# First projection tiles, the z stores and the gated unit's buffers in a two-layer decoder trunk

## The chip, the core and the metric

The kernel runs on one core of one Trainium2 chip. The metric is the device time of one execution in microseconds (us); lower is better.

## The reference, cut to what matters

x is 1024 positions by 1024 channels. Layer 0 is a state-space layer, layer 1 is differential attention:

```
xn = rmsnorm(x, g);  u, z = split(xn @ in_w)          # in_w: 1024 x 2048, u columns first
y  = s5_ssm(u, ...) + d_skip * u                       # 64 groups of 16 channels, 64 complex states each
y  = gelu(y)
y  = y * sigmoid(y @ glu_w + glu_b)                    # the gated unit
h  = x + (y * silu(z)) @ out_w
# layer 1: keys and values from h, queries and gate from h, attention, out-projection, final norm
```

The scan needs u. z is read only behind the gated unit, so it can be computed and stored at any time before.

## The kernel before, in words

Everything is held transposed: 128 channels on the partitions, 1024 positions along the free dimension, in 8 tiles (`KT`). A float32 product is split into three matmuls (`mm3`, lines 159 to 161): a rounded high part and a rest of each operand, hi*hi, hi*lo and lo*hi. A tile of a dense projection (`dense`) is 8 steps of k by two halves of 512 positions by 3, that is 48 matmuls into two PSUM banks. The pool `ps` has four banks, `ps2` two. Weights come by `load_m`: SyncE loads 512 KB into `mraw` (one buffer), ScalarE rounds them into `mhi` (line 749), VectorE takes the difference `mlo` (line 750); `mhi` and `mlo` have two buffers each.

The program is written as straight code and a planner orders the instructions of each engine at build time, by the order of the text, the buffers that are free, and its own estimate of each duration. Each engine and each DMA queue then runs its list in order.

Layer 0 begins with three tiles for which the weights come in pieces (`fw`), so that matmuls can start k by k while x arrives. Beside them run the sums of squares for the norm: matmuls of line 526, a ScalarE copy (530), small matmuls (532), `rcol` (534, 535), `norm_rows` (688) and a ScalarE copy into R (537). The norm is applied on evacuation: for tiles of u, VectorE multiplies the accumulator by R (line 491) and SyncE stores it (492). Tiles of z are copied as they are by ScalarE (494) and stored by SyncE (495); R comes in later, in the gated unit. Both go through `evo`, a ring of two buffers.

Then `ssm_setup` computes tables on VectorE (C3, B3, D, ES3, ET4 in pool `ssm`). `ORDER` lists the scan stage in the text's order: for each of the 8 groups of tiles, t and c make tables (`bt`, `bT`, `ca`, `toep`), u projects a tile, a feeds the scan (`ug`, `pb`), o computes y and ScalarE's queue stores it to `yd` (439). The tiles of z stand at the end of the text, and the planner takes them as filler. The gated unit (`glu`) loads y back (`load_y`, line 595): y0 early into a buffer of its own, y1 to y7 into `yr`, which uses the stream buffers tagged "ya", "sg" and "z", two of each. It casts them to `yh` (610) and `yl` (611), multiplies by `glu_w`, and its `done` reads z and y again and writes `y2h` and `y2l`. `yh` and `yl` take the memory of `xh` and `xl`. In memory the pool of y2 came first, above it the stream buffers `cd`, then `cd1`, where the pools of the scan stage had been.

Of the kernel before, what the change touches and what calls it, by code (L numbers as in the profile page):

```python
# [8 lines left out]
F32 = mybir.dt.float32  # L9
# [9 lines left out]
P = 128  # L19
SEQ = 1024  # L20
D = 1024
KT = D // P
# [11 lines left out]
NEG = -1e30  # L34


ORDER = ("t0 c0 t1 u3 a0 c1 o0 t2 u4 a1 c2 o1 t3 u5 a2 c3 o2 t4 u6 a3 c4 o3 t5 u7 a4 c5 o4 t6 a5 c6 o5 t7 a6 c7 o6 a7 "
         "o7").split()


# [14 lines left out]
class Trunk:  # L55
# [389 lines left out]
    def layer0(self, dbg=None):  # L445
        tc, nc, I = self.tc, self.nc, self.I
        V, G, S = nc.vector, nc.gpsimd, nc.scalar
        dr = self.dr
        ps = self.ps
# [9 lines left out]
        with ExitStack() as es:  # L459
            sp, ev = pool(es, "ssm", 1), pool(es, "ev", 2)  # L460
            stp = ExitStack()
            tp = pool(stp, "stp", 1)
            R = self.R1
            pcr = self.ps3.tile([P, 2, 512], F32, name="pb")
            sqs = []

            pick = tp.tile([P, 2], F32, name="pick")
            G.memset(pick, 0.0)
            for r in range(4):
                G.memset(pick[32 * r:32 * r + 1, r // 2:r // 2 + 1], 1.0)  # L470

            ga = tp.tile([P, KT], F32, name="ga")
            nc.sync.dma_start(ga, I["ga"])

            def prep_x(k, cuts):
                raw = tp.tile([P, SEQ], F32, name="xraw", bufs=3)
                g = ga[:, k:k + 1]
                for c in cuts:
                    nc.sync.dma_start(raw[:, c], I["xT"][k * P:(k + 1) * P, c])
                    S.activation(xh[k][:, c], raw[:, c], AF.Copy, scale=g)  # L480
                    V.scalar_tensor_tensor(xl[k][:, c], raw[:, c], g, rd(xh[k][:, c]), op0=ALU.mult,
                                           op1=ALU.subtract)
                sqs.append(tp.tile([P, SEQ], F32, name="rt0", bufs=3))
                S.activation(sqs[k], raw, AF.Square)

            def evac(m, pt):
                for h in range(2):
                    hs = slice(h * 512, h * 512 + 512)
                    o = ev.tile([P, 512], F32, name="evo")
                    if m < KT:  # L490
                        V.tensor_mul(o, pt[h], R[:, hs])  # L491
                        nc.sync.dma_start(udv[m][:, hs], o)
                    else:
                        S.copy(o, pt[h])
                        nc.sync.dma_start(zds[m - KT][:, hs], o)


            pt0 = [[(ps if m < 2 else self.ps2).tile([P, 512], F32, name="ps") for h in range(2)] for m in range(3)]
            fst = ExitStack()
            fp = pool(fst, "first", 1)  # L500
            fw = []
            for k in range(KT):
                raw = fp.tile([P, 3 * P], F32, name="fw", bufs=3)
                hi = fp.tile([P, 3 * P], F32R, name=f"fh{k}")
                lo = fp.tile([P, 3 * P], F32R, name=f"fl{k}")
                nc.sync.dma_start(raw, I["in_w"][k * P:(k + 1) * P, 0:3 * P])
                S.copy(hi, raw)
                V.tensor_sub(lo, raw, rd(hi))
                prep_x(k, (slice(0, 512), slice(512, SEQ)) if k == 0 else (slice(0, SEQ),))
                if k == 0:  # L510
                    self.load_consts()
                    for i, pl in enumerate((tp, sp)):
                        self.load_small(i, pl.tile([P, CUTS[i + 1] - CUTS[i]], F32, name=f"small{i}"))
                fw.append((hi, lo))
            def first_u(k):
                for m in range(3):
                    ms = slice(m * P, (m + 1) * P)
                    self.mm_tile((fw[k][0][:, ms], fw[k][1][:, ms]), pt0[m], xh, xl, k)

            late = KT - 2  # L520
            for k in range(KT):
                if k < late:
                    first_u(k)
                for h in range(2):
                    r = 64 * h + k % 2 * 32
                    nc.tensor.matmul(pcr[r:r + 32, 0, :], self.ones.broadcast_to([P, 32]),
                                     sqs[k][:, h * 512:h * 512 + 512], start=k < 2, stop=k >= KT - 2,
                                     tile_position=(0, r))
            part = tp.tile([P, SEQ], F32, name="rt0", bufs=3)[:, 0:512]
            S.copy(part, pcr[:, 0, :])  # L530
            for q in range(KT):
                nc.tensor.matmul(pcr[:, 1, q:q + 1], part[:, q % 4 * P:(q % 4 + 1) * P], pick[:, q // 4:q // 4 + 1],
                                 start=True, stop=True)
            S.activation(self.rcol, pcr[:, 1, 0:KT], AF.Identity, bias=self.small1[:, 5:6], scale=1.0 / D)
            G.tensor_tensor(self.rcol, self.rcol, self.mhalf.broadcast_to([P, KT]), op=ALU.pow)
            self.norm_rows([pcr[:, q // 4, q % 4 * P:(q % 4 + 1) * P] for q in range(KT)], self.rcol)
            S.copy(R, pcr.rearrange("p h c -> p (h c)"))
            for k in range(late, KT):
                first_u(k)
            fst.close()  # L540
            for m in range(3):
                evac(m, pt0[m])
            self.ssm_setup(sp, tp)
            V.memset(self.small1[:, 2:3], SUBLN_EPS)
            V.tensor_scalar(self.small1[:, 0:1], self.sm("subln"), 1.0 - LAM_INIT, None, op0=ALU.mult)
            V.tensor_scalar(self.gq, self.sm("gb"), 0.125, None, op0=ALU.mult)
            stp.close()
            yst = ExitStack()
            yq = yst.enter_context(tc.tile_pool(name="yq", bufs=YQ, side="right", reuse_waits="tile"))
            sb, tb = pool(es, "ssb", 2), pool(es, "sst", 1)  # L550
            self.ks = tb.tile([P, T, P], F32, name="ks")
            G.memset(self.ks, 0.0)
            psb = self.ps3
            t = {}
            ops = {
                "t": lambda b: t.update({b: self.ssm_in(b, sb, tb, self.ps2)}),
                "c": lambda b: self.ssm_tables(b, t[b], sb, tb, self.ps2, dr),
                "u": lambda b: self.dense(I["in_w"], (b,), xh, xl, ps, evac),
                "a": lambda b: self.ssm_apply(b, t[b], sb, tb, psb, uds[b]),
                "o": lambda b: self.ssm_out(b, t[b], tb, self.ps2, yds[b]),  # L560
            }
            for x in ORDER:
                ops[x[0]](int(x[1]))
            self.yraw = []
            for k in range(YQ):
                self.yraw.append(yq.tile([P, SEQ], F32, name="yq"))
                self.load_y(yds, k, self.yraw[k])
            self.dense(I["in_w"], range(8, 16), xh, xl, ps, evac)
        with ExitStack() as es:
            yp, cd, cd1 = pool(es, "y2p", 1), pool(es, "cd", 2), pool(es, "cd1", 1)  # L570
            self.glu(yp, cd, ps, yds, zds)
            yst.close()
            self.out0(cd, cd1, ps)
# [8 lines left out]
            hs = slice(h * 512, h * 512 + 512)  # L582
            self.mm3(pt[h], w[0], w[1], xh[k][:, hs], xl[k][:, hs], k == 0, k == KT - 1)

    def dense(self, src, tiles, xh, xl, ps, done, gain=None):

        for m in tiles:
            wh, wl = self.load_m(src, 0, KT, m * P, P, gain)
            pt = [ps.tile([P, 512], F32, name="ps") for h in range(2)]
            for k in range(KT):  # L590
                self.mm_tile((wh[:, k, :], wl[:, k, :]), pt, xh, xl, k)
            done(m, pt)
# [4 lines left out]
    def glu(self, yp, cd, ps, yds, zds):  # L597
# [19 lines left out]
        def done(m, pt):  # L617
            z = cd.tile([P, SEQ], F32, name="z")
            nc.sync.dma_start(z, zds[m])
            sg = cd.tile([P, SEQ], F32, name="sg")  # L620
            a = cd.tile([P, SEQ], F32, name="ya")
            self.load_y(yds, m, a)
            G.tensor_mul(z, z, self.R1)
            G.tensor_mul(a, a, z)
            S.activation(z, z, AF.Sigmoid)
            for h in range(2):
                hs = slice(h * 512, h * 512 + 512)
                S.activation(sg[:, hs], pt[h], AF.Sigmoid, bias=self.sm("glub")[:, m:m + 1])
            V.tensor_mul(sg, sg, z)
            V.tensor_mul(sg, sg, a)  # L630
            S.copy(self.y2h[m], sg)
            V.tensor_sub(self.y2l[m], sg, rd(self.y2h[m]))

        self.dense(I["glu_w"], range(8), yh, yl, ps, done)

    def out0(self, cd, cd1, ps):
        nc, I = self.nc, self.I
# [541 lines left out]
```

## Time and profile before

| | us |
|---|---|
| median of 3 runs (1092.6 to 1092.8) | 1092.7 |
| the profiled execution, its own time | 1093.5 |
| its span, first to last instruction | 1091.7 |
| TensorE busy | 1061.9 |
| VectorE busy | 822.5 |
| ScalarE busy | 623.9 |
| GpSimd busy | 235.3 |
| granted TensorE clock, mean | 0.991 |

The span is the time between the first and the last instruction on the core; the execution's own time has 1.8 us around it. In the rows, PE is TensorE, DVE VectorE, ACT ScalarE, POOL GpSimd, SPq and ACTq the queues by which SyncE and ScalarE issue transfers. L491 is line 491 of the kernel. Busy times of matmuls overlap, so steps between their starts are the better measure. A wait for several things is put down to the one that came last.

### The profile page before, as it was taken

What the parts mean: (1) busy time and instruction counts of PE and PEld (TensorE: products, weight loads), DVE (VectorE), ACT (ScalarE), POOL (GpSimd) and SP (SyncE); (2) the same over time, 40 slices, a digit from 0 to 9 for tenths busy, and PEclk for the clock granted to TensorE, in tenths of its full rate; (3) what the DMA queues carried; (4) which work ended last, traced back from release to release, by engine and by line L of the source; (5) the groups of instructions that cost most, each with busy time, mean ns of one, the idle gap of its engine ahead of it and who ended that gap; (6) DMA issues with size and microseconds to landing.
All of it is one profiled execution on the core that took longest, in us unless ns stands there. A gap on an engine that the chain in (4) does not pass through costs nothing. (4 is left out here: it accounts for less than half of the span.)

```text
span 1091.7 us, 17715 instructions
## 1 busy us (share of the span) xinstructions
PE 1061.9 (97%) x6308; PEld 908.2 (83%) x6308; DVE 822.5 (75%) x1617; ACT 623.9 (57%) x1396; POOL 235.3 (22%) x237
## 2 busy tenths in 40 slices
PE   7999999999999999999999999999999999899996
PEld 5678888887788888998888898889988898788896
DVE  7789999984577543547898778877698777987475
ACT  6432343332534332436787788767788778785463
POOL 0000000000356112211222122221222222210258
PEclk9999999999899999999999999999999999999998
DMA  8143546544654445313122212222222222553344
GB/s 283 45 136 116 174 151 174 159 151 133 238 193 135 127 140 157 135 42 90 44 85 57 73 56 66 86 56 78 66 53 79 60 84 61 148 175 105 109 134 159
DMA packets 143143, 125.94 MB, mean 115 GB/s; under 512 B 9808, under 2 KB 123216, under 8 KB 143056
## 3 DMA queue, kind: packets, MB, share of 16 engines
q1 hardware_dynamic: 134736, 120.63, 36.0%
q10 hardware_dynamic: 8320, 4.19, 1.3%
q8 instruction: 49, 0.80, 0.3%
q14 instruction: 38, 0.31, 0.1%
HBM read 85.48 MB, written 33.03 MB: 109 GB/s over the span
## 5 line engine op out<-in xcount | busy, mean ns | idle before, releaser
L159 PE MATMUL pm<-h1h,mhi 128*128 128x512 f32 x352 | 139.5, 396 | 1.0 <-DVE xr L767 1.0
L160 PE MATMUL pm<-h1l,mhi 128*128 128x512 f32 x352 | 138.8, 394 | 0.0
L161 PE MATMUL pm<-h1h,mlo 128*128 128x512 f32 x352 | 138.6, 394 | 0.0
L848 ACT ACTIVATE e<-e,tiny 128x256 f32<-128x256 f32 (+7 forms) x128 | 99.3, 777 | 33.6 <-DVE tiny L846 32.5
L846 DVE CUSTOM_DVE_ANT_0 e<-s,tri 128x256 f32<-128x256 f32 (+7 forms) x128 | 94.8, 750 | 11.9 <-PE s L841 6.3
L750 DVE TENSOR_TENSOR mlo<-mraw,mhi 128x1024 fp32r<-128x1024 f32 (+1 forms) x44 | 59.9, 1360 | 42.7 <-ACT mhi L749 42.5
L749 ACT CAST mhi<-mraw 128x1024 fp32r<-128x1024 f32 (+1 forms) x44 | 45.3, 1030 | 76.0 <-PE ps L160 55.0
L159 PE MATMUL ps<-xh,mhi 128*128 128x512 f32 x208 | 82.2, 395 | 1.9 <-DVE evo L491 1.9
L161 PE MATMUL ps<-xh,mlo 128*128 128x512 f32 x208 | 81.9, 394 | 0.0
L160 PE MATMUL ps<-xl,mhi 128*128 128x512 f32 x208 | 81.7, 393 | 0.0
L159 PEld LDWEIGHTS pm<-h1h,mhi 128*128 128x128 f32 x352 | 66.2, 188 | 14.7 <-DVE xr L767 2.4
L161 PEld LDWEIGHTS pm<-h1h,mlo 128*128 128x128 f32 x352 | 66.2, 188 | 12.7
L771 POOL TENSOR_TENSOR xs<-xs,RS 128x512 f32<-128x512 f32 x32 | 42.9, 1340 | 156.0 <-DMA xs<-ze 114.2
L160 PEld LDWEIGHTS pm<-h1l,mhi 128*128 128x128 f32 x352 | 66.2, 188 | 12.2
L840 PE MATMUL s<-k,q 128*128 128x384 f32 (+4 forms) x192 | 67.9, 356 | 3.0 <-DMA q<-z 3.0
L915 POOL TENSOR_TENSOR ob<-ob,sq 128x256 f32<-128x256 f32 x32 | 25.7, 803 | 190.3 <-ACT sq L910 177.9
L841 PE MATMUL s<-k,z 128*128 128x384 f32 (+4 forms) x192 | 65.9, 346 | 0.0
L810 PE MATMUL pm<-mhi,h1h 128*128 128x256 f32 x224 | 64.5, 288 | 1.1 <-DVE z L698 0.8
L735 ACT ACTIVATE mhi<-mraw,small 128x128 fp32r<-128x128 f32 (+1 forms) x152 | 51.8, 414 | 21.5 <-PE ps L160 14.4
L811 PE MATMUL pm<-mlo,h1h 128*128 128x256 f32 x224 | 63.3, 284 | 0.1
L812 PE MATMUL pm<-mhi,h1l 128*128 128x256 f32 x224 | 63.1, 283 | 0.0
L877 DVE TENSOR_TENSOR pl<-t,ph 128x512 fp32r<-128x512 f32 (+2 forms) x112 | 54.9, 492 | 10.8 <-ACT ph L876 10.4
(375 smaller groups left out, 3091.0 us busy)
## 6 DMA issues: line engine op xcount, KB each, us to landing
mraw<-in_kv_w SPq DMA_DIRECT2D x16, 512.0 KB
mraw<-in_b_in_w SPq DMA_DIRECT2D x16, 512.0 KB
mraw<-in_in_w SPq DMA_DIRECT2D x13, 512.0 KB
ud<-evo SPq DMA_DIRECT2D x16, 256.0 KB
ug<-ud SPq DMA_DIRECT2D x8, 512.0 KB
kd<-ks SPq DMA_DIRECT2D x8, 512.0 KB
toep<-kd SPq DMA_DIRECT2D x8, 512.0 KB
yd<-yb ACTq DMA_DIRECT2D x8, 512.0 KB
```

The costliest lines, as they stand in the source:

```text
L159: mm(ps, wh, xh, start=first, stop=False)
L160: mm(ps, wh, xl, start=False, stop=False)
L161: mm(ps, wl, xh, start=False, stop=last)
L750: nc.vector.tensor_sub(lo, raw, rd(hi))
L810: mm(o, self.h1h[k][:, ts], wh, start=k == 0, stop=False)
L811: mm(o, self.h1h[k][:, ts], wl, start=False, stop=False)
L812: mm(o, self.h1l[k][:, ts], wh, start=False, stop=k == KT - 1)
L840: mm(sps[m][:, c, :w], q2[m][:, qt], ks[m][:, cs], start=True, stop=False)
L841: mm(sps[m][:, c, :w], q2[2 + m][:, qt], ks[m][:, cs], start=False, stop=True)
L846: V.tensor_tensor_reduce(out=blocks(em[:, :L]), in0=sp[:, 0:nb, :w], in1=blocks(self.tri[:, SEQ - L:]), scale=-1.0, scalar=3e38, op0=ALU.a ...
L848: S.activation(em[:, :L], em[:, :L], AF.Exp, bias=nmx[:, m:m + 1], scale=-1.0, accum_out=sm[:, m:m + 1])
L877: V.tensor_sub(pl[:, jj, ii, :], tp[:, jj, ii, :], rd(ph[:, jj, ii, :]))
```

## The change

The first three tiles are tiles 0 to 2 of z where they were tiles 0 to 2 of u, and all of their matmuls and their evacuation stand ahead of the norm's small matmuls in the text. u0 follows by itself as a normal dense tile, u1 and u2 stand in `ORDER`, and the z tiles at its end are five. z is stored by ScalarE's queue. The pools `cd` and `cd1` are opened ahead of the pool of y2, so they lie lower. `dense` can begin several tiles together (`first`): all steps of k but the last for each, then the last step for each, then the evacuations; the gated unit does so for its first two tiles.

```diff
-ORDER = ("t0 c0 t1 u3 a0 c1 o0 t2 u4 a1 c2 o1 t3 u5 a2 c3 o2 t4 u6 a3 c4 o3 t5 u7 a4 c5 o4 t6 a5 c6 o5 t7 a6 c7 o6 a7 "
+ORDER = ("t0 c0 u1 t1 u2 a0 c1 o0 t2 u3 a1 c2 o1 t3 u4 a2 c3 o2 t4 u5 a3 c4 o3 t5 u6 a4 c5 o4 t6 u7 a5 c6 o5 t7 a6 c7 o6 a7 "
...
                         S.copy(o, pt[h])
-                        nc.sync.dma_start(zds[m - KT][:, hs], o)
+                        nc.scalar.dma_start(zds[m - KT][:, hs], o)
...
-                nc.sync.dma_start(raw, I["in_w"][k * P:(k + 1) * P, 0:3 * P])
+                nc.sync.dma_start(raw, I["in_w"][k * P:(k + 1) * P, D:D + 3 * P])
...
-            late = KT - 2
             for k in range(KT):
-                if k < late:
-                    first_u(k)
+                first_z(k)
                 for h in range(2):
...
+            fst.close()
+            for m in range(3):
+                evac(KT + m, pt0[m])
             part = tp.tile([P, SEQ], F32, name="rt0", bufs=3)[:, 0:512]
...
-            for k in range(late, KT):
-                first_u(k)
-            fst.close()
-            for m in range(3):
-                evac(m, pt0[m])
+            self.dense(I["in_w"], (0,), xh, xl, ps, evac)
             self.ssm_setup(sp, tp)
...
-            self.dense(I["in_w"], range(8, 16), xh, xl, ps, evac)
+            self.dense(I["in_w"], range(11, 16), xh, xl, ps, evac)
         with ExitStack() as es:
-            yp, cd, cd1 = pool(es, "y2p", 1), pool(es, "cd", 2), pool(es, "cd1", 1)
+            cd, cd1, yp = pool(es, "cd", 2), pool(es, "cd1", 1), pool(es, "y2p", 1)
...
-    def dense(self, src, tiles, xh, xl, ps, done, gain=None):
-
-        for m in tiles:
+    def dense(self, src, tiles, xh, xl, ps, done, gain=None, first=0):
+
+
+        begun = []
+        for m in tiles[:first]:
+            wh, wl = self.load_m(src, 0, KT, m * P, P, gain)
+            begun.append((m, wh, wl, [ps.tile([P, 512], F32, name="ps") for h in range(2)]))
+        for ks in (range(KT - 1), (KT - 1,)):
+            for m, wh, wl, pt in begun:
+                for k in ks:
+                    self.mm_tile((wh[:, k, :], wl[:, k, :]), pt, xh, xl, k)
+        for m, wh, wl, pt in begun:
+            done(m, pt)
+        for m in tiles[first:]:
...
-        self.dense(I["glu_w"], range(8), yh, yl, ps, done)
+        self.dense(I["glu_w"], range(8), yh, yl, ps, done, first=2)
```

## Rows read from the trace of the kernel before

**Rows 1.** The page: an engine's busy time, share of the span, instructions.

```profile
PE 1061.9 (97%) x6308; PEld 908.2 (83%) x6308; DVE 822.5 (75%) x1617; ACT 623.9 (57%) x1396; POOL 235.3 (22%) x237
```

**Rows 2.** TensorE's waits, whole span: line, what ended it, total, times, longest.

```profile
PE ps L159 <- ACT yh L610: 4.3, 1, 4.3
...
PE ps L159 <- DVE evo L491: 1.9, 1, 1.9
...
PE ps L362 <- DVE ca L311: 0.5, 2, 0.3
```

**Rows 3.** Windows: busy time (instructions) per engine, granted clock, DMA share, GB/s.

```profile
55.80:60.00 4.20, 4.20 (x19) 3.47 (x20) 1.99 (x9) 0.03 (x1) 0.00 (x0) 1.00 0.36 129
...
128.00:225.00 97.00, 96.72 (x802) 79.75 (x801) 94.68 (x93) 32.59 (x82) 2.79 (x13) 1.00 0.52 158
...
271.40:275.60 4.20, 0.00 (x0) 0.00 (x0) 0.00 (x0) 1.04 (x1) 0.00 (x0) 0.76 0.92 317
275.60:280.50 4.90, 4.85 (x12) 3.83 (x13) 4.76 (x4) 4.01 (x4) 0.00 (x0) 0.51 1.03 405
```

**Rows 4.** TensorE in order of time: start, duration, line, tile [idle before <-what ended it].

```profile
51.89 1.95 PE L688 MATMUL pb<-ident,rcol 128*128 128x128 f32 x16
55.74 0.50 PE L159 MATMUL ps<-xh,mhi 128*128 128x512 f32 x1 [1.91 <-DVE evo L491]
...
268.31 0.39 PE L159 MATMUL ps<-yh,mhi 128*128 128x512 f32 x1
...
270.12 0.39 PE L159 MATMUL ps<-yh,mhi 128*128 128x512 f32 x1
...
275.65 2.07 PE L159 MATMUL ps<-yh,mhi 128*128 128x512 f32 x4 [4.25 <-ACT yh L610]
```

**Rows 5.** ScalarE in order of time.

```profile
42.48 0.59 ACT L530 COPY rt<-pb 128x512 f32<-128x512 f32 x1 [8.23 <-PE pb L526]
...
53.96 1.00 ACT L537 COPY R<-pb 128x1024 f32<-128x1024 f32 x1
...
267.30 0.37 ACTq L439 DMA_DIRECT2D yd<-yb  x1
267.82 0.59 ACT L494 COPY evo<-ps 128x512 f32<-128x512 f32 x1 [0.55 <-PE ps L161]
...
274.55 1.04 ACT L610 CAST yh<-yr 128x1024 fp32r<-128x1024 f32 x1 [4.71 <-DMA yr<-yd]
...
293.12 0.69 ACT L628 ACTIVATE sg<-ps,glub 128x512 f32<-128x512 f32 x1 [0.81 <-PE ps L161]
293.71 1.04 ACT L749 CAST mhi<-mraw 128x1024 fp32r<-128x1024 f32 x1
```

**Rows 6.** VectorE in order of time.

```profile
54.99 1.29 DVE L491 TENSOR_TENSOR evo<-ps,R 128x512 f32<-128x512 f32 x2 [6.23 <-ACT R L537]
...
60.00 0.69 DVE L491 TENSOR_TENSOR evo<-ps,R 128x512 f32<-128x512 f32 x1 [2.14 <-DMA ud<-evo]
...
71.02 1.21 DVE L311 TENSOR_TENSOR bt<-w,w 128x1024 f32<-128x1024 f32 x1
...
238.78 1.23 DVE L311 TENSOR_TENSOR ca<-w,w 128x1024 f32<-128x1024 f32 x1
...
294.78 2.38 DVE L750 TENSOR_TENSOR mlo<-mraw,mhi 128x1024 fp32r<-128x1024 f32 x1 [8.30 <-ACT mhi L749]
...
464.31 0.70 DVE L938 TENSOR_TENSOR RC<-RC,R 128x512 f32<-128x512 f32 x1 [0.76 <-ACT R L679]
```

**Rows 7.** Transfers that SyncE issues, in order of time.

```profile
268.43 1.75 SPq L495 DMA_DIRECT2D zd<-evo  x2
270.28 3.12 SPq L595 DMA_DIRECT2D yr<-yd  x6
...
451.02 0.33 SPq L651 DMA_DIRECT2D h1d<-sg  x1
```

**Rows 8.** SyncE's waits in 255 to 290 us.

```profile
SPq L495 <- ACT evo L494: 12.8, 3, 10.6
```

More of the change, by code (lines that the diff above doesn't have):

```diff
@@ L514, in layer0, with first_z @@
                 fw.append((hi, lo))
-            def first_u(k):
+            def first_z(k):
                 for m in range(3):
```

## Prediction

> **What bounds the kernel now.** I read the page first: TensorE (PE) is busy for 1061.9 us of a span of 1091.7 [rows 1]. A kernel like that can only be shortened by less matmul work, which this change doesn't touch, or by closing holes in TensorE's row. So the second view is TensorE's waits, longest first [rows 2]. The reader is to see that the list is short, and that two of its entries lie where the diff works: 4.3 us for `yh` (line 610, start of the gated unit) and 1.9 us for `evo` (line 491, evacuation of the first u tiles). Third come windows around these two holes, for the granted clock [rows 3], and then the timelines of the engines that end the waits [rows 4 to 8].
>
> **The first hole** is 1.91 us before the matmul at 55.74 [rows 4]. VectorE's evacuation of u0 multiplies by R, and R is copied out by ScalarE only at 53.96 [rows 5]; VectorE had stood idle for 6.23 us in front of it [rows 6]. All six accumulators of the first three tiles are full till then, so the fourth tile has no PSUM to start in.
>
> **The second hole** is 4.25 us before the matmul at 275.65 [rows 4], and it has a tail. In 271.4 to 275.6 the granted clock falls to 0.76, in the next 4.9 us it is 0.51, the lower of its two levels (1.2 against 2.4 GHz). After the 1.91 us hole it stayed at 1.00 [rows 3]. At 0.51 the stretch gives 4.9 x 0.49 = 2.4 us less than at full clock. The Trainium skill (TensorE: Matmul & The Clock Gate, HAM oscillation) says the same in kind: idle gaps that are long enough put the array back to its lower rate and work has to earn the upper one again; by it only the longer hole is followed by a slow stretch, and these rows agree.
>
> What ends the second hole is a ScalarE cast at 274.55 that waited for a load `yr<-yd` [rows 5]. That load left SyncE at 270.28, directly behind two stores `zd<-evo` that began at 268.43 [rows 7], and the longest of the waits of these stores for ScalarE's copy was 10.6 us [rows 8]. So the loads of y stood in a first-in-first-out queue behind stores of the last z tile. The load itself took 274.55 - 270.28 = 4.3 us to be usable.
>
> **The change part by part.**
>
> *First tiles of z.* z's evacuation is a plain ScalarE copy, without R. A half takes 0.59 us (line 494, the same copy behind the last z tile [rows 5]). The tiles are computed k by k, so z0 is complete 12 matmuls before z2. A step between matmuls is (270.12 - 268.31) / 8 = 0.226 us [rows 4], so that is 2.7 us, against two copies, 1.2 us. u0 can start in z0's accumulators when z2 ends, and the matmuls of the R chain are further filler. I take 1.91 us off, bounds 0 and 1.91. New cost: the ring of `evo` has two buffers, and the third copy has to wait for a store; VectorE waited 2.14 us for that before [rows 6]. Now ScalarE waits, with the R chain's copies and those of D behind it. Nothing on TensorE needs R before u0 is evacuated. TensorE's last R matmuls ended at 51.89 + 1.95 = 53.84 [rows 4]; with the same work ahead of it and no hole, u0's 48 matmuls of 0.226 us end near 64.7. From ScalarE's copy of the sums to the end of R's copy it took 53.96 + 1.00 - 42.48 = 12.5 us with deferred matmuls between [rows 5], so a chain that starts when the z tiles end, near 50, gives R by 62.5. The cost is nothing; without that cover it is at most those 2.14 us twice.
>
> *u0 by itself, order of the rest.* The 13 dense tiles behind the first three are still 13, so TensorE's filler for the scan stage is equal. What moves is VectorE: it is 97.6% busy in 128 to 225 [rows 3] and is the scan's own limit. It gets back 6.23 + 2.14 us of standing idle early, and has three more u evacuations later in place of the early ones. u0 now arrives later, which is the slower rival below. I take zero.
>
> *z stored by ScalarE's queue.* 16 issues at 0.37 us (that of `yd` [rows 5]) are 5.9 us of ScalarE, spread over the scan stage where it is about a third busy. SyncE's queue loses 16 stores that wait for a copy. The Trainium skill (DMA: Bandwidth & Descriptors, Issuing engines are not separate DMA queues) speaks against a gain here: transfers of all queues share the same 16 engines, and a second issuer saves only the issue time. By that the store move alone would give next to nothing. The rows show another thing, an in-order wait of up to 10.6 us [rows 8], and it decides.
>
> *Buffers lower.* Before, the stream buffers ("ya", "sg", "z", 24 KB a partition) lay above 64 KB of y2, by my sum of the tile sizes over the scan's `toep`, `ug` and `v`, which o7 reads until ScalarE stores its result at 267.30 [rows 5]. Now they start where the setup tables (C3, B3, D, ES3, ET4, 31 KB) lay. The last to read those is c7, whose `ca` is written at 238.78 [rows 6] and whose matmuls follow at once. So six of the seven loads can leave some 25 us earlier, and y1 to y6 can be cast as the last z tile gives up xh and xl. TensorE would go from z15 into the gated unit without a hole: 4.25 + 2.4 us off, bounds 0 and 6.65. Further on, layer 1's RC and RS now overlie "sg" instead of y2h. The last tile's store of `sg` leaves at 451.02 [rows 7] and RC is multiplied at 464.31 [rows 6]. A load of 4.3 us behind it has 9 us to spare: nothing.
>
> *First two gated tiles together.* Matmuls for k = 0 to 6 of both tiles come before either's k = 7. That gives 84 matmuls x 0.226 = 19 us in which the last y may come. But both tiles end 1.4 us apart, all four accumulators and both weight buffers with them. The third tile needs an evacuation (0.69) and its weights cast (1.04 [rows 5]) and split (2.38 beside GpSimd [rows 6]). The cast fits into the second tile's 1.4 us within some tenths; the split is needed only by every third matmul, and the planner may put the others first. Bounds: 0, and 0.69 + 1.04 + 2.38 - 1.4 = 2.7 us. I take 0.6, nearest to the case of a cast just in time. Before, the first tile's evacuation began at 293.12 and TensorE ran on.
>
> *A new plan.* Orders are drawn anew on every engine. The remaining small waits, such as the 0.5 us for `ca` [rows 2], may grow or go: 0, with 1 us either way.
>
> **Sum** against the profiled execution (1093.5 us for a span of 1091.7, 0.8 us over the median): -1.91 - 4.25 - 2.4 + 0.6 = -7.96, so 1085.5; on the median of 1092.7, **1084.7 us**.
>
> **The rivals.**
> - *The wait for y stays in part.* The loads are early but the plan, or casts and splits of ScalarE and VectorE in a row, leave a hole. For it: the y loads still share SyncE with `toep` and weight loads that wait. Against: up to 25 us of room. A hole half as long, at full clock, gives 1084.7 + 2.1 = 1086.8; the whole one 1084.7 + 6.65 = 1091.4, which is within the 0.2% (2.2 us) that a measurement of this kernel can tell from no change. Chance 0.13, 0.05 of it for the whole hole.
> - *The pair runs dry.* Tile three starts late by the 2.7 us bound, or by more if ScalarE has z's sigmoid in front, long enough to lose the clock: 2.7 + 2.4 - 0.6 = 4.5 us, 1089.2. The Trainium skill (Perfetto Trace Analysis, Optimizing Tensor Performance) has the rule for it: independent groups should rotate through banks, so that one is evacuated under the next one's matmuls; two groups ending together break that, and no run so far shows it here. Chance 0.10; in 0.02 of it the stall comes again at later tiles and eats the gain.
> - *The scan is late (slower).* u0's tile ends near 64.7, where its evacuation began at 54.99 [rows 6]. With 1.3 us of multiplication and two transfers of at most 4.3 us it is usable by 75; a0's other input, from `bt` at 71.02 + 1.21 [rows 6], is ready no earlier than 72 now. So u0 can hold the chain by 3 us, if VectorE takes it without delay. y7, stored at 267.30, has about 7 us to spare (two transfers and a cast and split, 11 us, in the 19 us, started some 2 us earlier). The kernel gets slower only if the chain comes 15 us later: 7 to use up the margin, 8 for the gain. At 20 us it would be 1084.7 + 13 = 1098. Chance 0.06.
>
> **How the numbers follow.** My forecast has 0.71; its own range is 1083 (no handover cost, small waits gone) to 1086.5. The 8-in-10 range reaches into the first two rivals: 1083.0 to 1089.5. Faster by over 0.2%: 0.71 + 0.08 + 0.08 = 0.87. Within 0.2%: 0.05 + 0.02 = 0.07. Slower: 0.06.
>
> **What would show it.** Right: no wait of TensorE for `evo` near 52 us; `yr` loads issued at some 242 to 262 us; granted clock 1.00 from z15 through the gated unit's first tiles; `zd` issues on ScalarE. Wrong: a TensorE wait for `mhi`, `mlo` or `sg` at the third gated tile; `yr` loads still directly before their casts; TensorE waiting for scan matmuls between 60 and 260.

## The result and the profile after

The changed kernel takes **1086.6 us** (median, 1084.9 to 1087.6) against 1092.65 (1092.4 to 1092.8) for the kernel before on the same chip: ratio 0.9943, interval 0.9926 to 0.9960. A second series of the same kernel gave 1086.3, ratio 0.9942 (0.9926 to 0.9958). So it is faster by some 6 us, by more than the 0.2% that can be told from no change, and it lies 1.9 us above the forecast of 1084.7. The profiled execution took 1086.2 for a span of 1084.3.

The page's line on TensorE and the first lines of TensorE's waits, to hold against [rows 1, 2]:

```profile
PE 1059.3 (98%) x6308; PEld 905.7 (84%) x6308; DVE 824.7 (76%) x1617; ACT 624.0 (58%) x1396; POOL 235.3 (22%) x237
```

```profile
PE ps L159 <- ACT xh L480: 7.1, 1, 7.1
...
PE ps L362 <- DVE ca L311: 0.8, 1, 0.8
```

The two entries the forecast was built on are gone: no wait for `yh`, none for `evo`. Two others have grown: the one for `ca` (0.5 in [rows 2], now 0.8), and the first, which is the start of the kernel: TensorE's first matmul comes at 7.06 where it came at 5.96.

The windows (columns as in [rows 3]):

```profile
55.80:60.00 4.20, 4.20 (x28) 3.78 (x27) 0.00 (x0) 3.57 (x8) 0.00 (x0) 1.00 0.12 44
128.00:225.00 97.00, 96.17 (x766) 79.46 (x768) 95.16 (x97) 30.27 (x75) 2.37 (x12) 1.00 0.49 152
264.00:285.00 21.00, 21.00 (x125) 17.66 (x124) 8.92 (x6) 8.51 (x10) 10.42 (x4) 1.00 0.71 227
285.00:290.00 5.00, 5.00 (x24) 4.15 (x23) 0.24 (x1) 1.00 (x2) 0.00 (x0) 1.00 0.00 0
290.00:300.00 10.00, 10.00 (x44) 7.83 (x43) 8.81 (x8) 5.32 (x7) 1.89 (x1) 1.00 0.66 218
```

In 264 to 285, where the kernel before had its 4.25 us hole, TensorE is busy for 21.00 of 21.00 at a granted clock of 1.00. It stays so in 285 to 300, where the third gated tile follows the pair.

SyncE's loads of y, to hold against the six at 270.28 in [rows 7]:

```profile
249.40 2.40 SPq L603 DMA_DIRECT2D yr<-yd  x3
252.33 0.97 SPq L603 DMA_DIRECT2D yr<-yd  x2
263.87 0.32 SPq L603 DMA_DIRECT2D yr<-yd  x1
...
279.64 0.32 SPq L603 DMA_DIRECT2D yr<-yd  x1
```

Five leave some 20 us earlier, the sixth at 263.87. The last, that of y7, leaves at 279.64. ScalarE's timeline shows why, and the z copies:

```profile
48.12 0.58 ACT L494 COPY evo<-ps 128x512 f32<-128x512 f32 x1 [12.56 <-PE ps L161]
48.73 0.33 ACTq L495 DMA_DIRECT2D zd<-evo  x1
...
50.81 0.59 ACT L494 COPY evo<-ps 128x512 f32<-128x512 f32 x1 [1.12 <-DMA zd<-evo]
...
270.88 1.09 ACT L437 ACTIVATE yb<-ps 128x512 f32<-128x512 f32 x2 [0.40 <-ACT evo L494]
...
275.71 1.06 ACT L633 ACTIVATE z<-z 128x1024 f32<-128x1024 f32 x1 [2.44 <-POOL ya L632]
275.72 0.38 ACTq L439 DMA_DIRECT2D yd<-yb  x1
...
282.93 1.05 ACT L618 CAST yh<-yr 128x1024 fp32r<-128x1024 f32 x1 [1.32 <-DMA yr<-yd]
...
289.58 1.04 ACT L757 CAST mhi<-mraw 128x1024 fp32r<-128x1024 f32 x1
```

y7 is computed at 270.88 + 1.09 = 271.97, but its store stands in ScalarE's list behind z's sigmoid, which waits for GpSimd, and is issued only at 275.72; before, it was issued at 267.30 [rows 5].

**Where the time came from.** I added up TensorE's timeline to the first matmul on `y2h` (the out-projection), which starts at 362.28 before and at 356.45 after. The steps between starts were summed by tile, the holes apart:

| us | before | after | difference |
|---|---|---|---|
| first matmul | 5.96 | 7.06 | +1.10 |
| hole for `evo` | 1.91 | 0 | -1.91 |
| hole for `yh` | 4.25 | 0 | -4.25 |
| other holes (`ca`; before, 0.17 of it for `yb`) | 0.63 | 0.83 | +0.20 |
| steps of the gated unit's matmuls | 89.72 | 87.57 | -2.15 |
| sums of squares, 32 matmuls | 6.89 | 7.86 | +0.97 |
| rest | | | +0.21 |
| first matmul on `y2h` | 362.28 | 356.45 | -5.83 |

The span is 7.4 us shorter; the other 1.6 us lie behind that matmul, in the out-projection and layer 1, whose code is the same. There TensorE has a hole for `q` (3.00 us before, 2.62 after, 3.18 in the second series), and what follows it differs from run to run: in 940 to 950 and 950 to 960 the clock was 1.00 and 0.83 before, 0.88 and 0.95 after, and 1.00 and 1.00 in the second series. This may be part of why single times of one kernel spread by 2 to 4 us; no run takes it by itself.

### The profile page after: what moved, and what is told of

It is laid out like the page before. It is cut to its first block, busy times and chain, and to the rows that moved or that the text cites. A ratio compares the mean times of both kernels' runs of the same rounds, so it can differ in the third digit from the quotient of the medians.

```text
span 1084.3 us, 17704 instructions
## 1 busy us (share of the span) xinstructions
PE 1059.3 (98%) x6308; PEld 905.7 (84%) x6308; DVE 824.7 (76%) x1617; ACT 624.0 (58%) x1396; POOL 235.3 (22%) x237
## 5 line engine op out<-in xcount | busy, mean ns | idle before, releaser
L758 DVE TENSOR_TENSOR mlo<-mraw,mhi 128x1024 fp32r<-128x1024 f32 (+1 forms) x44 | 62.8, 1428 | 29.7 <-ACT mhi L757 29.3
```

What stands on the lines that cost most here:

```text
L758: nc.vector.tensor_sub(lo, raw, rd(hi))
```

## The experiments

The theory was that of the prediction: SyncE's first-in-first-out queue, with z's stores in it, holds the loads of y, and their place in memory matters next to it. The rival: the tiles of memory alone hold them. Ratios are to the kernel before on the same chip, with 95% intervals.

**e1, the queue alone.**

```diff
-                        nc.sync.dma_start(zds[m - KT][:, hs], o)
+                        nc.scalar.dma_start(zds[m - KT][:, hs], o)
```

> The kernel before, with only the z stores moved to ScalarE's queue. By the prediction's step on SyncE's order the loads of y leave when o7 frees their buffers, near 267 instead of 270.3 us: TensorE's hole ahead of the gated unit shrinks from 4.3 to some 1 to 2 us, the clock stays, and the median is near 1088. Rival, memory decides and the copy of the last z tile was no real limit: the loads leave within 1 us of before, the hole and the slow clock stay, 1092 to 1093.

Measured: 1095.1 us, ratio 1.0033 (1.0020 to 1.0045). SyncE's loads and TensorE's waits:

```profile
265.85 10.94 SPq L595 DMA_DIRECT2D yr<-yd  x6
```

```profile
PE ps L159 <- ACT mhi L749: 2.2, 1, 2.2
PE ps L161 <- DVE mlo L750: 1.9, 1, 1.9
PE ps L159 <- DVE evo L491: 1.9, 1, 1.9
PE ps L159 <- ACT yh L610: 1.4, 2, 1.1
```

SyncE's waits for these loads in 255 to 285 us, and ScalarE's list at the holes for `mhi` and `mlo`:

```profile
SPq L595 <- PE ps L424: 8.8, 1, 8.8
SPq L595 <- DMA yd<-yb: 7.7, 1, 7.7
```

```profile
291.54 1.06 ACT L625 ACTIVATE z<-z 128x1024 f32<-128x1024 f32 x1 [4.72 <-POOL ya L624]
292.51 0.67 ACT L628 ACTIVATE sg<-ps,glub 128x512 f32<-128x512 f32 x1
293.08 1.03 ACT L749 CAST mhi<-mraw 128x1024 fp32r<-128x1024 f32 x1
```

With the queue free of z's stores, the loads begin at 265.85, when o7's last matmuls (line 424) end: 4.4 us earlier than before, as the prediction's step had it, and no more. Five of the six leave in a row; the sixth waits another 7.7 us, until the last store from `yb` has landed. TensorE's wait for `yh` falls from 4.3 to 1.4 us, but the next tile's weights are cast hardly sooner: at 293.08 (293.71 before [rows 5]), behind a sigmoid that waits for GpSimd. So TensorE then stands for `mhi` and `mlo`, and the holes come to 5.5 us in all. The queue had held the loads, by some 4 us; ahead of that their memory holds them, and the queue alone gains nothing.

**e2, the lower buffers alone.**

```diff
-            yp, cd, cd1 = pool(es, "y2p", 1), pool(es, "cd", 2), pool(es, "cd1", 1)
+            cd, cd1, yp = pool(es, "cd", 2), pool(es, "cd1", 1), pool(es, "y2p", 1)
```

> The kernel before, with only the stream buffers lower in memory (z still stored by SyncE). If SyncE's order is what held the loads, some of them stay behind the stores of the last z tiles and a hole of 1 to 4 us is left: 1087 to 1091. Rival, memory decides alone: loads of y1 to y5 leave near 243 to 252 us, no hole, clock 1.00, near 1086 (1092.7 less 4.25 and 2.3).

Measured: 1086.35 us, ratio 0.9949 (0.9937 to 0.9961): as much as the whole change. SyncE's loads, with z's stores in their old queue:

```profile
241.38 1.27 SPq L595 DMA_DIRECT2D yr<-yd  x3
243.56 2.31 SPq L595 DMA_DIRECT2D yr<-yd  x2
255.68 0.32 SPq L595 DMA_DIRECT2D yr<-yd  x1
271.52 0.32 SPq L595 DMA_DIRECT2D yr<-yd  x1
```

With their memory free earlier, the planner puts five loads ahead of the stores of the last two z tiles. No hole for `yh`, clock 1.00 in 264 to 285; the 1.91 us for `evo` stay. One line gives the gain.

**e3, both.** The two diffs above.

> The kernel before, with both: z stored by ScalarE, buffers lower, but u tiles first and no pair of gated tiles. Both theories: no hole for y1 to y6, so 1092.7 - 4.25 - 2.3 = 1086.1. If the last y is late for the first gated tile without the pair, TensorE waits for the cast of y7 by 1 to 4 us some 10 us after it began the gated unit: 1087 to 1091.

Measured: 1086.4 us, ratio 0.9943 (0.9929 to 0.9956). The queue adds nothing to the buffers.

**e4, the change without the pair.**

```diff
-        self.dense(I["glu_w"], range(8), yh, yl, ps, done, first=2)
+        self.dense(I["glu_w"], range(8), yh, yl, ps, done)
```

> The changed kernel without the pair of first gated tiles. In the changed kernel y7 was cast only at 282.9 us, since ScalarE's queue issued its store at 275.7. Without the pair the first tile's last step stands some 35 matmuls = 8 us earlier in TensorE's list: if that is right it waits some 4 to 6 us for y7 and loses the clock after it, 1091 to 1095, so the pair is what keeps the gain. Rival, the plan's filler covers y7 as it did in the kernel before: within 1 us of the changed kernel, 1086 to 1087.5.

Measured: 1090.9 us, ratio 0.9987 (0.9976 to 0.9998). TensorE's timeline:

```profile
283.97 0.73 PE L159 MATMUL ps<-yh,mhi 128*128 128x512 f32 x2 [2.15 <-ACT yh L618]
```

The first gated tile reaches k = 7 before y7 is cast, and TensorE stands for 2.15 us; the clock stayed at 1.00 behind it. The first matmul on `y2h` is 2.0 us later than in the changed kernel. The medians differ by some 4.5; what the other 2.5 are, this profile doesn't settle (from that matmul on it is 1.8 us longer).

**e5, the new order alone.** The changed kernel with SyncE's z stores, the old order of the pools and no pair.

> The kernel before, with only the new order: z tiles first, u0 by itself, u1 and u2 in the scan's order (z stored by SyncE, buffers high, no pair). By the prediction the 1.91 us hole goes whole: 1092.2 - 1.9 = 1090.3, with the hole ahead of the gated unit left. By what the changed kernel's trace shows, its place is taken by 1.0 us of sums of squares that no longer stand side by side on TensorE, 0.6 us more waiting for ca and a start up to 1 us later: within 1 us of the kernel before, 1091 to 1093, or above it if y7, later by 3 us or more, widens the second hole.

Measured: 1095.6 us, ratio 1.0033 (1.0022 to 1.0045): slower. TensorE's timeline and the window behind the hole:

```profile
278.32 2.08 PE L159 MATMUL ps<-yh,mhi 128*128 128x512 f32 x4 [5.34 <-ACT yh L618]
```

```profile
278.30:284.00 5.70, 5.68 (x16) 4.57 (x17) 5.45 (x5) 4.51 (x5) 0.00 (x0) 0.62 1.07 379
```

The hole for `evo` is gone, and that for `yh` is 1.1 us longer, again with a slow stretch behind it.

**e6, the change once more**, as the base of the runs beside it.

> The changed kernel as it is, for a second trace of its start and as the neighbour of the next run. Median near 1086.6; the first matmul near 7 us if the z columns are what arrives later, near 6 us if the first trace's 7.06 was chance.

Measured: 1086.3 us, as told above.

**e7, sums of squares of two blocks side by side.** The 32 small matmuls come four to a k, on two strips of 32 output columns; odd k use two other strips. In the kernel before, the groups of two k stood next to each other once, and the eight took 1.06 us where four take 1.05. The change's new order runs all of them one k at a time. So, in the changed kernel:

```diff
-            for k in range(KT):
-                first_z(k)
-                for h in range(2):
...
+            for k2 in range(0, KT, 2):
+                made = first_z(k2)
+                made += first_z(k2 + 1)
+                self.in_order(made[-1:] + [nc.tensor.matmul(
+                    pcr[64 * h + k % 2 * 32:64 * h + k % 2 * 32 + 32, 0, :], self.ones.broadcast_to([P, 32]),
...
+                    tile_position=(0, 64 * h + k % 2 * 32)) for k in (k2, k2 + 1) for h in range(2)])
```

> The changed kernel with the sums of squares of an even and the next odd tile kept next to each other on TensorE (they write four different strips of 32 columns). In the traces four such matmuls alone take 0.98 us and the one group of eight of the kernel before took 1.0 us. If strips overlap, the 32 matmuls take 4.0 instead of 7.9 us: 3.9 us off, near 1082.7. Rival, the group of eight was cheap for another reason, or the later sums hold up the ring of squares and x arrives later: 1085.5 to 1087.

Measured: **1080.7 us, ratio 0.9900 (0.9881 to 0.9919)**, faster than both kernels. The sums in TensorE's timeline, first of the changed kernel (8 groups), then of this one (4 groups):

```profile
13.83 1.05 PE L524 MATMUL pb<-rt,small 128*32 128x512 f32 x4
14.82 1.67 PE L159 MATMUL ps<-xh,fh 128*128 128x512 f32 x6
```

```profile
17.34 1.06 PE L525 MATMUL pb<-rt,small 128*32 128x512 f32 x8
18.33 1.67 PE L159 MATMUL ps<-xh,fh 128*128 128x512 f32 x6
```

Four take 14.82 - 13.83 = 0.99 us, eight 18.33 - 17.34 = 0.99. The sums fall from 7.86 to 3.98 us, and the first matmul on `y2h` comes at 351.06, against 355.59 in e6. That is 4.5 us, and the medians differ by 5.6; the sums account for 3.9 of it, and what the rest is, no run shows.

**e8, the same sums with only the buffers lower**, u first as in the kernel before.

> The kernel before with lower buffers (as in the run with that part alone) and the sums of squares side by side as far as the plan lets them (groups of 8, 8, 12 and 4): the 32 matmuls take some 4.5 to 5 instead of 6.9 us, so 2 us off the run with lower buffers alone: near 1084.4. If z tiles first are worth their 1.91 us, the changed kernel with paired sums is faster than this by 1 us or more; if they only pay for their own side costs, this one is level with it.

Measured: 1087.8 us, ratio 0.9962 (0.9949 to 0.9976), no better than e2. TensorE's waits and three windows:

```profile
PE pb L690 <- POOL rcol L535: 2.2, 1, 2.2
PE ps L159 <- DVE evo L491: 1.8, 1, 1.8
```

```profile
50.00:56.00 6.00, 3.06 (x16) 2.76 (x16) 2.54 (x10) 3.48 (x8) 1.66 (x1) 0.74 0.00 0
52.03:55.08 3.05, 3.05 (x16) 2.76 (x16) 2.31 (x8) 0.57 (x2) 0.00 (x0) 0.64 0.00 0
56.00:60.00 4.00, 3.08 (x7) 2.48 (x8) 2.81 (x6) 1.58 (x5) 0.00 (x0) 0.50 0.37 130
```

With u first, all accumulators wait for R, so a shorter sum stage leaves TensorE nothing to do while R's chain runs: two holes of 2.15 and 1.83 us close together. The clock falls behind the first one already: 0.64 in 52.03 to 55.08, which lies between the holes, and 0.50 behind the second. With z first (e7) u0's tile covers that chain.

**e9, the change with z's stores in SyncE's queue again** (e1's diff backwards).

> The changed kernel with the z stores issued by SyncE again; the lower buffers, the pair and the new order stay. Theory, memory decides: the loads of y0 to y7 need their tiles of memory and nothing of the z copies, because with z first these copies come at some 48 us or later, tile by tile, and the ones behind the last z tile only gate what SyncE issues after them. The first yr loads stay near 249 us, y7's at about 280, and the time is 1086.3 within 1.5 us. Rival, the queue matters once memory is free: SyncE stands at each z store until ScalarE has copied, the yr loads issue 5 us or more later, TensorE waits for y7 or y6 by 1 to 4 us, and the time is 1088 to 1092.

Measured: 1087.2 us, ratio 0.9957 (0.9942 to 0.9973), not to be told from the change. The first `yr` loads leave at 249.49, y7's at 282.10, 2.5 us later than with the change. TensorE's timeline here, and VectorE's split of y7 in the changed kernel:

```profile
288.59 0.50 PE L160 MATMUL ps<-yl,mhi 128*128 128x512 f32 x1 [0.76 <-DVE yl L619]
```

```profile
284.01 1.23 DVE L619 TENSOR_TENSOR yl<-yr,yh 128x1024 fp32r<-128x1024 f32 x1 [10.59 <-ACT yh L618]
```

ScalarE's list in e9, at y7:

```profile
275.89 1.06 ACT L633 ACTIVATE z<-z 128x1024 f32<-128x1024 f32 x1 [1.74 <-POOL ya L632]
278.27 0.60 ACT L437 ACTIVATE yb<-ps 128x512 f32<-128x512 f32 x1
278.90 0.37 ACTq L439 DMA_DIRECT2D yd<-yb  x1
```

TensorE wanted y7 at 288.59 - 0.76 = 287.83. In the changed kernel it is split by 284.01 + 1.23 = 285.24, so the pair has some 2.6 us to spare if TensorE wants y7 at the same time there. The z stores on ScalarE's queue are worth no time. Whether they are worth that margin is not shown: the new plan of e9 computes the second half of y7 behind z's sigmoid, at 278.27, where the changed kernel has it done by 271.97.

**e10, the change with the old order of the pools** (e2's diff backwards).

> The changed kernel with the y buffers in their old place in memory; the queue, the pair and the order stay. Theory, memory decides: the yr loads issue no earlier than about 265 us, TensorE has a hole of 2 us or more in front of the first product on y, in part bridged by the pair, and the time is 1091 to 1096. Rival, the pair and the free queue do it without the lower buffers: loads near 250 us and a time of 1087 or less.

Measured: 1095.7 us, ratio 1.0028 (1.0017 to 1.0039). SyncE's loads and TensorE's hole:

```profile
271.17 3.28 SPq L603 DMA_DIRECT2D yr<-yd  x6
```

```profile
277.84 2.08 PE L159 MATMUL ps<-yh,mhi 128*128 128x512 f32 x4 [6.38 <-ACT yh L618]
```

Queue, pair and order together, without the buffers, are slower than the kernel before.

**e11, the first piece of weights from other columns.**

```diff
-                nc.sync.dma_start(raw, I["in_w"][k * P:(k + 1) * P, D:D + 3 * P])
+                c0 = D if k else 0
+                nc.sync.dma_start(raw, I["in_w"][k * P:(k + 1) * P, c0:c0 + 3 * P])
```

> The changed kernel with the first weight piece alone (rows 0 to 127) read from the u columns 0 to 383 in place of the z columns, so the products of the first eighth of the sum over z tiles 0 to 2 are made with other weights. Theory, the address of the columns sets how late the first piece lands: ScalarE's first cast of fw starts at 4.2 to 4.4 us and the first matmul at 5.9 to 6.2, as in the kernels that begin with u. Rival, something else of the new program (its length, the order of its first transfers): the cast stays at 5.0 to 5.2 us and the first matmul at 7.0.

Measured, one run: 1084.3 us. In the first eighth of k it has other weights than z's, so it serves for the time alone. ScalarE's first cast of `fw`, in this run and in the changed kernel:

```profile
4.37 0.51 ACT L508 CAST fh<-fw 128x384 fp32r<-128x384 f32 x1 [2.15 <-DMA fw<-in_in_w]
```

```profile
5.14 0.51 ACT L507 CAST fh<-fw 128x384 fp32r<-128x384 f32 x1 [2.92 <-DMA fw<-in_in_w]
```

The load is issued at 1.21 us here and at 1.18 in the changed kernel. The first matmul is back at 6.16, and the fourth tile starts at 51.20 where it started at 52.50. The cast starts at 4.2 to 4.3 us in the five kernels that begin with the u columns, at 4.8 to 5.2 in the seven that load the z columns as second transfer. So the columns matter; why those land later, no run shows. The place in the queue counts too: issued first, at 0.74, the z columns are cast at 4.08 (e12), 3.3 us after their issue, where it takes 3.6 to 4.0 us in those seven.

**e12, e7 with the first piece ahead of `ga`.**

```diff
-            nc.sync.dma_start(ga, I["ga"])
...
                 nc.sync.dma_start(raw, I["in_w"][k * P:(k + 1) * P, D:D + 3 * P])
+                if k == 0:
+                    nc.sync.dma_start(ga, I["ga"])
```

> The changed kernel with the sums of squares of two blocks side by side, and SyncE's first two issues exchanged: the first weight piece ahead of the gains ga. Theory, the first piece's landing sets the start: it is issued 0.4 us earlier, the first cast starts at 4.6 to 4.8 us and the first matmul 0.2 to 0.5 us earlier than 7.09, and the time is 1080.3 within 1 us, not to be told from 1080.7. Rival, x's load or ga sets the start: the first matmul stays at 7.0 to 7.2 or moves later, and the time is 1080.7 to 1081.5.

Measured: 1080.4 us, ratio 0.9893 (0.9876 to 0.9911), not to be told from e7. The piece is issued at 0.74, cast at 4.08, and the first matmul comes at 5.59, 1.5 us earlier than in e7, three times what was expected. At the fourth tile 0.55 of that is left (46.58 against 47.13), at the first matmul on `y2h` 0.3: the early stages run at the pace of what else arrives, and two small waits (0.41 and 0.66) come back later.

## Why the prediction came out as it did

- **The first hole** (-1.91) closed as worked out: z0's copy at 48.12 needs no R, and u0 starts right behind z2. The third copy did wait for a store (1.12 us on ScalarE), with nothing behind it that TensorE needed.
- **The second hole and its slow stretch** (-4.25 and -2.4) closed with the clock at 1.00; the gated unit's steps fell by 2.15. The size was right and the cause was not; the forecast of the time held because the diff has both edits. "An in-order wait of up to 10.6 us [rows 8], and it decides" is the step that failed: the wait for ScalarE's copy was on SyncE's row, but it held the loads by only some 4 us, and ahead of that they had nowhere to go. e1 takes the wait away and gains nothing; e2 moves the buffers, leaves z's stores in SyncE's list and gains all; e9 and e10 say the same from the other end. The Trainium skill (DMA: Bandwidth & Descriptors, Issuing engines are not separate DMA queues), by which a second issuer saves only issue time, was the better guide here: the times of e1, e3 and e9 agree with it.
- **The pair** (+0.6): the handover cost nothing, 5.00 of 5.00 and 10.00 of 10.00 us busy around it. The third tile's cast comes only at 289.58, but TensorE had the second tile's matmuls until then and the high parts to go on with. The pair's use was greater than I thought. I gave y7 some 7 us to spare with its store on time; with the store 8.4 us later it still had some 2.6 (e9). Without the pair TensorE waits (e4).
- **The slower rival** stood nearer than its 0.06 looked. The scan's last `ca` is written at 245.10 where it was at 238.78 [rows 6], and y7's store leaves 275.72 - 267.30 = 8.4 us later, of which 3.75 are the wait behind z's sigmoid in ScalarE's list, which I had not counted. The margin took it up.
- **What was missed**, and makes the 1.9 us: +0.97 for sums of squares no longer side by side, +1.10 for the later start (e11), +0.2 for `ca` and +0.2 in small steps. Up to the out-projection the holes and the slow stretch came to -8.31 against -8.56 forecast, the pair to 0 against +0.6, and what was not foreseen to +2.5: -5.8, where -7.96 was forecast. The medians moved by -6.1.

So of the four edits one makes the time, the buffers' place. The new order wins 1.9 us and gives it back at the start and in the sums; it delays y7, and the pair mends that. With the sums paired as well, the kernel with the order, the queue and the pair is faster than the one without these three (e7 against e8); the order by itself was not tried there.

## What to carry to other kernels

When a transfer leaves late behind a wait in its queue, look for when its target's memory came free before blaming the queue: move the buffer, or move the queue, one at a time. A closed hole is a gain only as far as what ran side by side in the old order still does; here small matmuls that had shared the array were pulled apart and ate 1 of 6 us. An edit that frees an early stage is worth what the stages behind it can take over, so its companions (the pair, the paired sums) decide whether it pays.

## What the runs showed of the hardware that was not expected

- Matmuls of 32 output columns on four different strips take together as long as on two: 8 in 0.99 us, 4 in 0.99 (e7). The Trainium skill (TensorE: Matmul & The Clock Gate, Part 3: Packing small matmuls) says that small matmuls on distinct column groups run at the same time; these rows agree, at 0.99 us for either count.
- The same load of 128 x 384 values, issued at the same moment, was usable some 0.4 to 1.0 us later from columns 1024 on (cast at 4.80 to 5.19, seven runs) than from column 0 (4.22 to 4.37, six runs).
- How long a hole was did not settle what the clock did behind it. The holes of 4.25 [rows 3, 4], 5.34 (e5) and 6.38 us (e10, clock 0.76 in the 6.16 us behind it) were followed by a slow stretch, and that of 1.91 us [rows 3, 4] was not. In between it went either way: a hole of 2.15 us kept the clock in e4 (1.00) and lost it in e8 (0.64 in the 3.05 us behind it), and the hole for `q` in layer 1, 3.18 us long in both e4 and e6, was followed by 0.82 in 951.62 to 960 in e4 and by 1.00 in 947.24 to 957 in e6. So the prediction's reading, that only the longer hole loses the clock, holds for its two holes and goes no further.
